# Set-up of a hybrid GLA and attention step: two weight bounds moved from VectorE to ScalarE, one row pass moved to GpSimd, set-up keys set anew

## The chip, the cores and the metric

The kernel runs on one core of one Trainium2 chip. The metric is the device time of one execution in microseconds (us). The engines are TensorE (PE, with its weight loads listed as PEld), VectorE (DVE), ScalarE (ACT), GpSimd (POOL) and SyncE (SP), which only issues transfers here.

## The reference

One inference step of two layers at model width 1024, over 256 context tokens and 1024 latent tokens. Layer 0 is a gated linear attention, layer 1 a softmax attention with grouped queries. All arithmetic is float32. Only the start of layer 0 matters here:

```python
hp = rms_norm(xp, norm_g[l]) * (1.0 + sc_p) + sh_p      # context rows
hs = rms_norm(xs, norm_g[l]) * (1.0 + sc_s) + sh_s      # latent rows

def gla_mixer(h, w_in, wa1, wa2, ba, onorm, w_out, s0):
    proj = h @ w_in
    q, k, v, gate = jnp.split(proj, [...], axis=-1)
    ...
    def decay(d):
        z = ((h @ wa1[d]) @ wa2[d] + ba[d]).astype(jnp.float32)
        return (jax.nn.log_sigmoid(z) / GLA_TAU).reshape(B, T, GLA_HEADS, GLA_DK)
```

## The kernel before

Every float32 operand of a large matmul is split into two float16 parts, hi and lo, and a product is made of three matmuls. Before a weight is split it is scaled by a power of two. That scale comes from a bound on the weight's magnitudes: the largest magnitude of each partition (`tensor_reduce` on DVE, into a small tile `wmx`), then the largest over all partitions by a small matmul on PE and a reduction of its result (`pow2`, result `p2m`, then `p2c`, `p2e`, the scale `p2s` and its inverse `p2i`).

The set-up works on three groups of row tiles of 128 tokens (`GROUPS`): four latent tiles, four more, and the two of the context. For a group, the rows' sums of squares are taken (`normalise`: a Square with an accumulator on ACT, or a product with an accumulator on DVE), POOL raises them to the power -1/2 (`rstd`, L238), the rows are scaled, PE transposes them, and ACT, DVE and POOL multiply by the conditioned gain, add the shift and split the result into `hT_hi` and `hT_lo` (`modulate`). PE then multiplies by the query and key weights of head 0 (`qk_pair`) and by the first low-rank weight (`rank`, then `rank_sum`). Names in the code: `ys` are the rows of the second group (tiles `x`), `zs` those of the context (in the buffer of `whi`, with their modulated rows in that of `wlo`), `w1` and `w2` the low-rank weights (both in one `wada` tile, split into `wa1h`, `wa1l` and `wa`), `vf` the first value weight (in `wst`), split by `fill`.

The loop over heads and row tiles (`gla`) follows, in which the value and gate products, the decays, the chunk products and the scans are interleaved, and then the attention.

A scheduler writes each engine's order. It takes the instructions by priority, and `LATER` adds a number to the priority of a named step (`later`, `placed`): negative is earlier. Names with `s.` belong to the set-up: `s.rk` splits the low-rank weights, `s.n1` normalises the second group, `s.m1` transposes and modulates it, `s.q0` and `s.q1` are the query and key products of the first and second group, `s.r0` and `s.r1` the low-rank products, `s.s0` and `s.s1` their sums, `s.v` splits the first value weight, `s.n2` normalises the context rows. All transfers into the chip that the set-up uses are issued in order on SP's queue, those of `w2` and `w1` at L585 and L587.

Of the kernel before, what the change touches and what calls it, by code (L numbers as in the profile page):

```python
# [9 lines left out]
F32 = mybir.dt.float32  # L10
I32 = mybir.dt.int32
AF = mybir.ActivationFunctionType
ALU = mybir.AluOpType
AX = mybir.AxisListType
# [3 lines left out]
P = 128  # L18
D = 1024
KT = D // P  # L20
# [6 lines left out]
GQ, GV = GH * DK, GH * DV  # L27
# [77 lines left out]
    "a0.q": 35,  # L105
    "wo3": 180,
    "x.key": -95,
    "s.v": 580,
    "s.q1": 185,
    "s.r0": -155,  # L110
    "s.n2": -490,
    "s.r1": 300,
    "gated9": 30,
    "eprep": 400,
    "x.kset": 170,
    "s.q0": -25,
    "s.s0": 45,
    "s.m1": -170,
    "s.s1": 245,
    "s.rk": -135,  # L120
    "s.n1": 0,
    "a9.val.3": -265,
    "a.s0.1": -55,
    "a9.val.1": -105,
# [36 lines left out]
class K:  # L161
# [136 lines left out]
                nc.vector.scalar_tensor_tensor(lo, par[:, q, :, b, :], so[:, b : b + 1], hi, ALU.mult, ALU.subtract)  # L298


    def fill(self, w, j, st):
        nc = self.nc
        s, w[2][j] = self.scale(st)
        h = KT // 4
        for i in range(4):
            a, n = slice(i * h, i * h + h), slice(256 * j, 256 * j + 256)
            hi, lo = w[0][:, a, n], w[1][:, a, n]
            act = nc.scalar.activation(hi, st[:, a, :], AF.Copy, scale=s)
            dve = nc.vector.scalar_tensor_tensor(lo, st[:, a, :], s, hi, ALU.mult, ALU.subtract)  # L309
        return act.ins, dve.ins  # L310
# [218 lines left out]
    def normalise(self, xs, junk, other=None):  # L529
        nc = self.nc  # L530
        n = len(xs)
        ssq = self.t(self.sm, [P, n], F32, f"nt_s{n}", bufs=2)
        for j, x in enumerate(xs):
            if other is not None and j % 2:
                nc.vector.scalar_tensor_tensor(
                    other, x, 1.0, x, ALU.mult, ALU.mult, accum_out=ssq[:, j : j + 1]
                )
            else:
                nc.scalar.activation(junk, x, AF.Square, accum_out=ssq[:, j : j + 1])
        r = self.rstd(ssq, D, f"nt_r{n}")  # L540
        for j, x in enumerate(xs):
            last = nc.vector.tensor_scalar(x, x, r[:, j : j + 1], None, ALU.mult)
        return last.ins

    def transpose(self, xs, k, tag):
# [49 lines left out]
        load(self.onorm, I["gla_onorm"].rearrange("l (j p) -> p (l j)", p=P))  # L595


    def split_rank(self, w1, w2):
        nc = self.nc
        mx = self.t(self.small, [P, 2], F32, "wmx")  # L600
        nc.vector.memset(mx, 0.0)
        nc.vector.tensor_reduce(mx[:, 0:1], w1, AX.XY, ALU.max, apply_absolute_value=True)
        nc.vector.tensor_reduce(mx[0:98, 1:2], w2, AX.XY, ALU.max, apply_absolute_value=True)
        s, inv = self.pow2(mx, 2)
        hi = self.t(self.gcp, [P, KT, 32], F16, "wa1h")
        lo = self.t(self.gcp, [P, KT, 32], F16, "wa1l")
        nc.scalar.activation(hi, w1, AF.Copy, scale=s[:, 0:1])
        nc.vector.scalar_tensor_tensor(lo, w1, s[:, 0:1], hi, ALU.mult, ALU.subtract)
        self.wa1 = hi, lo

        nc.scalar.activation(self.wa2, w2, AF.Copy, scale=s[0:98, 1:2])
        low = self.wa2[64:98]
        nc.vector.scalar_tensor_tensor(low, w2[64:98], s[64:98, 1:2], low, ALU.mult, ALU.subtract)
        nc.scalar.activation(self.wa2[96:97], w2[96:97], AF.Copy, scale=s[96:97, 1:2])
        self.inv_rank = self.t(self.gcp, [P, 2], F32, "inv_rk")
        nc.vector.tensor_copy(self.inv_rank, inv)

# [971 lines left out]
def run(job):  # L1589
    return job[0](*job[1:])  # L1590
# [3 lines left out]
def emit(ctx, tc, I, O, dbg=None, stop=None):  # L1594
    k = K(ctx, tc, I, O, dbg)
    nc = tc.nc
# [27 lines left out]
    with ExitStack() as c:  # L1624
# [9 lines left out]
        with ExitStack() as c1:  # L1634
            k.p1 = k.pool("p1", ctx=c1)
            k.hw = k.p1
            small = nc.scalar.dma_start
            rows = k.t(k.p1, [40, P], F32, "rows")
            small(rows[0:8, :], I["c_ctx"].rearrange("(k p) -> k p", p=P))
            small(rows[8:16, :], I["c"].rearrange("b (k p) -> (b k) p", p=P))  # L1640
            small(k.ident, I["k_ident"])
            small(rows[16:24, :], I["norm_g"][0].rearrange("(k p) -> k p", p=P))
            small(rows[24:40, :], I["b_ada"][0, 0 : 2 * D].rearrange("(k p) -> k p", p=P))

            def group(gi):
                xs = []
                for j in range(GROUPS[gi][1]):
                    x = k.t(k.p1, [P, D], F32, "x", bufs=4)
                    load(x, xrow(I, GROUPS[gi][0] + j))
                    xs.append(x)  # L1650
                return xs

            xs = group(0)
            wq = k.wtile(0)
            qk = k.load_qk(wq, 0)
            to = []
            for t in (*k.wtile(1)[0:2], *k.wtile(2)[0:2], k.hT_hi, k.hT_hi, k.hT_lo, k.hT_lo):
                a = 4096 * (len(to) % 2) if len(to) > 3 else 0
                t = t.rearrange("p k n -> p (k n)")[:, a : a + 4096].bitcast(F32)
                n = len(to)  # L1660
                for b in ((0, 2 * D),) if n < KT - 1 else ((0, D), (D, 2 * D)):
                    load(t[:, slice(*b)], I["w_ada0"][n, :, slice(*b)])
                to.append(t)
            w = k.gla_consts()
            k.cond_vectors(rows)
            junk = k.t(k.p1, [P, D], F16, "junk")
            last = k.normalise(xs, junk)
            xT = k.t(k.p1, [P, KT, 512], F32, "xT")
            for kk in range(KT):
                nc.vector.tensor_copy(xT[:, kk, :], k.transpose(xs, kk, ("z", "mm")[kk % 2]))  # L1670
            k.mod_rows(to[0:NEAR], 0)
            with tc.issue_after(last):
                run(qk)
                cross = k.cross
            k.gla_tables()
            ys = group(1)
            wv = k.wtile(1)
            vf = k.load_v(wv, 0)
            k.spare = k.bank("U")
            step = cross  # L1680
            for n in range(NEAR, KT):
                with tc.issue_after(step):
                    k.mod_rows(to[n : n + 1], n)
                if n < KT - 1:
                    step = k.idle_steps(6, k.mod_mm)
            k.mod_cols()
            step = k.idle_steps(6, k.mod_mm)
            late = [t.rearrange("p k n -> p (k n)").bitcast(F32) for t in k.wtile(2)[0:2]]
            zs = [late[0][:, D * j : D * j + D] for j in range(2)]
            for j, x in enumerate(zs):  # L1690
                load(x, xrow(I, GROUPS[2][0] + j))
            with tc.issue_after(step):
                k.gs, k.sh, k.inv_h = k.affine()
            step = k.idle_steps(16, k.cross)
            for kk in range(KT):
                act, dve = k.modulate(xT[:, kk, :], kk, GROUPS[0][0], kk % 2 == 0)
            k.fold_qk(0, wq)
            with tc.issue_after(act.ins), tc.issue_after(dve.ins):
                with k.later("s.rk"):
                    k.split_rank(*w)  # L1700
                    k.rank_scales()
                k.placed("s.n1", k.normalise, ys, junk, k.t(k.p1, [P, D], F16, "junk2"))
            with tc.issue_after(step):
                k.placed("s.q0", k.qk_pair, 0, 0, wq)
            nxt = k.placed("s.r0", k.rank, 0)
            with k.later("s.m1"):
                for kk in range(KT):
                    act, dve = k.modulate(
                        k.transpose(ys, kk, banks[kk % 6]), kk, GROUPS[1][0], kk % 2 == SECOND
                    )  # L1710
            first = dve.ins
            with tc.issue_after(act.ins), tc.issue_after(first):
                k.placed("s.v", run, vf)
                k.placed("s.n2", k.normalise, zs, junk)
            k.placed("s.q1", k.qk_pair, 0, 1, wq)
            k.placed("s.s0", k.rank_sum, *nxt)
            k.placed("s.s1", k.rank_sum, *k.placed("s.r1", k.rank, 1))
            late_qk = k.load_qk(wq, 1)
# [135 lines left out]
def xrow(I, i):  # L1854
    if i < NTP:
        return I["x_prompt"][0, i * P : i * P + P, :]
    return I["x_sample"][0, (i - NTP) * P : (i - NTP) * P + P, :]
# [97 lines left out]
```

## Time and profile before

| | us |
|---|---|
| median of 3 runs | 1243.88 (1243.77 to 1244.47) |
| the profiled execution | 1240.44 |
| its span, first to last instruction | 1238.7 |
| PE busy | 1190.6 (96%) |
| DVE busy | 941.7 (76%) |
| ACT busy | 684.6 (55%) |
| POOL busy | 323.7 (26%) |
| mean granted TensorE clock | 0.997 of full speed |

Times in the profile are counted from the span's start. A line such as L602 is one of the kernel before; in the new kernel the same statements stand 4 to 25 lines further down. A name on the left of an arrow is the tile written, those on the right are read. A PE row's end is modelled, so rows of PE that follow each other can overlap by a little.

### The profile page before, as it was taken

To read this page: it belongs to the slowest core of one execution; us is meant where nothing else is said; L and a number is where in the kernel's file an instruction comes from. 1 tells how busy PE (TensorE), PEld (TensorE's weight loads), DVE (VectorE), ACT (ScalarE), POOL (GpSimd) and SP (SyncE) were. 2 spreads that over 40 slices of the span, in tenths; PEclk is the share of its full clock that TensorE was granted. 3 is DMA by queue.
4 is the path that set the end of the run, shared out by engine and by line. 5 is a ranking of instruction groups with operands and counts; after the bars stand their busy time and mean duration, and the time that the engine had idled before them with its cause. 6 is when DMAs were issued, how large, how long until landed. Compare 5 with 4: busy or idle time off the path is not lost. (4 is left out here: it accounts for less than half of the span.)

```text
span 1238.7 us, 22382 instructions
## 1 busy us (share of the span) xinstructions
PE 1190.6 (96%) x7990; PEld 779.1 (63%) x7990; DVE 941.7 (76%) x2177; ACT 684.6 (55%) x1694; POOL 323.7 (26%) x566
## 2 busy tenths in 40 slices
PE   5899999999999999799999999999999999989998
PEld 3467765655556566567776666766766667766444
DVE  4787778888788789986876877877767687796653
ACT  3574565666666657742333576666677676663100
POOL 0132122333221243310223444331332342310000
PEclk9999999999999999999999999999999999999999
DMA  9511567366555544479987896667957666889442
GB/s 381 215 48 74 196 195 237 113 198 203 175 186 171 184 136 144 124 189 308 205 192 187 186 174 137 134 132 145 191 126 156 128 118 137 193 152 240 153 136 85
DMA packets 318496, 210.14 MB, mean 170 GB/s; under 512 B 257158, under 2 KB 294702, under 8 KB 310064
## 3 DMA queue, kind: packets, MB, share of 16 engines
q1 hardware_dynamic: 311232, 191.18, 60.2%
q10 hardware_dynamic: 4688, 10.57, 2.3%
q0 software_dynamic: 2464, 6.95, 2.0%
q8 instruction: 63, 1.03, 0.4%
q14 instruction: 49, 0.40, 0.1%
HBM read 108.35 MB, written 38.96 MB: 119 GB/s over the span
## 5 line engine op out<-in xcount | busy, mean ns | idle before, releaser
L247 PEld LDWEIGHTS <-hT_hi 128*128 128x128 f16 x1920 | 187.6, 98 | 119.9 <-issue 3.8
L247 PE MATMUL mm<-whi,hT_hi 128*128 128x512 f16 (+1 forms) x576 | 200.1, 348 | 3.1 <-ACT gx L718 2.7
L247 PE MATMUL mm<-whi,hT_lo 128*128 128x512 f16 (+1 forms) x576 | 200.2, 347 | 0.0
L247 PE MATMUL mm<-wlo,hT_hi 128*128 128x512 f16 (+1 forms) x560 | 194.2, 347 | 0.7 <-DVE wlo L309 0.7
L247 PEld LDWEIGHTS <-whi 128*128 128x128 f16 x1232 | 120.2, 98 | 60.3 <-issue 0.9
L1344 PE MATMUL S<-kT,wst 128*128 128x512 f16 (+1 forms) x624 | 142.1, 338 | 6.5 <-ACT p L1352 6.5
L247 PE MATMUL mm<-hT_hi,whi 128*128 128x256 f16 (+1 forms) x480 | 141.0, 294 | 0.6 <-DVE og L1407 0.6
L247 PE MATMUL mm<-hT_lo,whi 128*128 128x256 f16 (+1 forms) x480 | 141.0, 294 | 0.0
L247 PE MATMUL mm<-hT_hi,wlo 128*128 128x256 f16 (+1 forms) x480 | 141.0, 294 | 0.0
L1382 DVE SCALAR_TENSOR_TENSOR phl<-p,srec,phl 128x1280 f16<-128x1280 f32 (+1 forms) x79 | 105.5, 1335 | 45.7 <-ACT phl L1381 28.4
L247 PEld LDWEIGHTS <-hT_lo 128*128 128x128 f16 x960 | 94.2, 98 | 61.3 <-issue 0.9
L1347 DVE TENSOR_REDUCE smx<-S 128x1 f32<-128x1280 f32 (+1 forms) x80 | 101.5, 1272 | 27.3 <-PE S L1344 27.1
L247 PE MATMUL mm<-PT,vh 128*128 128x256 f16 x672 | 114.8, 273 | 5.8 <-DMA PT<-phl 5.6
L1352 ACT ACTIVATE p<-S,snb,acol 128x1280 f32<-128x1280 f32 (+1 forms) x80 | 99.0, 1238 | 8.9 <-DVE phl L1382 3.8
L1344 PEld LDWEIGHTS <-wst 128*128 128x128 f16 x624 | 61.0, 98 | 57.0 <-issue 7.7
L247 PE MATMUL mm<-PT,vl 128*128 128x256 f16 x336 | 91.6, 273 | 0.0
L1379 POOL TENSOR_SCALAR phl<-p,srec 128x1280 f16<-128x1280 f32 (+1 forms) x40 | 53.7, 1342 | 104.6 <-DVE srec L1370 57.8
L247 PEld LDWEIGHTS <-wlo 128*128 128x128 f16 x616 | 60.2, 98 | 29.4
L247 PEld LDWEIGHTS <-vh 128*128 128x128 f16 x672 | 65.2, 98 | 16.0 <-DMA PT<-phl 4.4
L1172 POOL TENSOR_TENSOR rope<-hx,ropet 128x64 f32<-128x64 f32 x160 | 53.9, 367 | 76.2 <-ACT hx L1308 61.9
L270 DVE TENSOR_REDUCE wmx<-wst 128x1 f32<-128x512 f32 x104 | 65.2, 677 | 7.4 <-DMA wst<-in_att_w 5.2
L238 POOL TENSOR_TENSOR hrs<-hrsa,mhalf 128x2 f32<-128x2 f32 x50 | 40.1, 803 | 102.8 <-DVE hrsa L236 84.9
(383 smaller groups left out, 2681.0 us busy)
## 6 DMA issues: line engine op xcount, KB each, us to landing
wada<-in_w_ada SPq DMA_DIRECT2D x16, 1024.0 KB, 5.4
wst<-in_att_w SPq DMA_DIRECT2D x14, 1024.0 KB, 5.5
wst<-in_gla_w_in SPq DMA_DIRECT2D x12, 1024.0 KB, 5.5
og_d<-og POOLq DMA_DIRECT2D x40, 128.0 KB, 2.8
wst<-og_d SPq DMA_DIRECT2D x5, 1024.0 KB, 6.5
og_d<-gx SPq DMA_DIRECT2D x37, 128.0 KB, 2.1
xr<-x_d SPq DMA_DIRECT2D x9, 512.0 KB, 3.4
out<-xr ACTq DMA_DIRECT2D x17, 256.0 KB, 2.0
```

What stands on the lines that cost most here:

```text
L238: nc.gpsimd.tensor_tensor(r, a, self.mhalf[:, 0:w], ALU.pow)
L247: self.pe = self.nc.tensor.matmul(out, a, b, start=k == 0 and j == 0, stop=k == n - 1 and j == 2).ins
L270: nc.vector.tensor_reduce(mx[:, j : j + 1], st[:, 2 * j : 2 * j + 2, :], AX.XY, ALU.max, apply_absolute_value=True)
L1172: nc.gpsimd.tensor_tensor(tv[:, h, :, w, :], xv[:, h, :, 1 - w, :], sn[:, :, w, :], ALU.mult)
L1344: nc.tensor.matmul(S[:, a : a + n], x, y, start=m == 0, stop=m == 2)
L1347: last = nc.vector.tensor_reduce(mx, S, AX.X, ALU.max).ins
L1352: nc.scalar.activation(p, S, AF.Exp, scale=self.sexp, bias=nb, accum_out=den)
L1379: nc.gpsimd.tensor_scalar(hi, p, r, 2.0 ** 14, ALU.mult, ALU.mult)
L1382: nc.vector.scalar_tensor_tensor(lo, p, r2, hi, ALU.mult, ALU.subtract)
```

## The change

The low-rank weights and the first value weight get their bound from ACT: it takes the absolute value with an accumulator, which gives each partition's sum of magnitudes instead of its largest. A sum is never smaller than the largest term, so it is a bound too. The low-rank bounds stand as a step of their own (`s.rb`), emitted ahead of the modulation of the first group; those of the value weight (`row_sums`, `s.vb`) are two sums that one DVE addition joins. In the second group POOL scales the third of four row tiles. The split of the second low-rank weight (`s.w2`) and the scales (`s.rs`) have keys of their own, and the keys of the set-up steps are set anew.

```diff
@@ LATER
-    "s.v": 580,
+    "s.v": 530,
...
+    "s.vb": 115,
+    "s.rb": 395,
...
+    def row_sums(self, st, junk):
+        mx = self.t(self.small, [P, 4], F32, "wmx")
+        h = KT // 2
+        for j in range(2):
+            f = st[:, h * j : h * j + h, :].rearrange("p k n -> p (k n)")
+            self.nc.scalar.activation(junk, f, AF.Abs, accum_out=mx[:, j : j + 1])
+        m = self.t(self.small, [P, 1], F32, "wm1")
+        self.nc.vector.tensor_tensor(m, mx[:, 0:1], mx[:, 1:2], ALU.add)
+        return m
+
-    def fill(self, w, j, st):
+    def fill(self, w, j, st, m=None):
         nc = self.nc
-        s, w[2][j] = self.scale(st)
+        s, w[2][j] = self.scale(st) if m is None else self.pow2(m)
...
         for j, x in enumerate(xs):
-            last = nc.vector.tensor_scalar(x, x, r[:, j : j + 1], None, ALU.mult)
+            if other is not None and j == 2:
+                nc.gpsimd.tensor_scalar(x, x, r[:, j : j + 1], 1.0, ALU.mult, ALU.mult)
+            else:
+                last = nc.vector.tensor_scalar(x, x, r[:, j : j + 1], None, ALU.mult)
...
+    def rank_bounds(self, w1, w2, junk):
+        nc = self.nc
+        mx = self.t(self.p1, [P, 2], F32, "rmx", bufs=1)
+        nc.gpsimd.memset(mx, 0.0)
+        for j, (t, n, w) in enumerate(((w1, P, 32 * KT), (w2, 98, 2 * GQ))):
+            f = t.rearrange("p a b -> p (a b)")
+            nc.scalar.activation(junk[0:n, 0:w], f, AF.Abs, accum_out=mx[0:n, j : j + 1])
+        self.rmx = mx
+
     def split_rank(self, w1, w2):
         nc = self.nc
-        mx = self.t(self.small, [P, 2], F32, "wmx")
-        nc.vector.memset(mx, 0.0)
-        nc.vector.tensor_reduce(mx[:, 0:1], w1, AX.XY, ALU.max, apply_absolute_value=True)
-        nc.vector.tensor_reduce(mx[0:98, 1:2], w2, AX.XY, ALU.max, apply_absolute_value=True)
-        s, inv = self.pow2(mx, 2)
+        s, inv = self.pow2(self.rmx, 2)
...
-        nc.scalar.activation(self.wa2, w2, AF.Copy, scale=s[0:98, 1:2])
-        low = self.wa2[64:98]
-        nc.vector.scalar_tensor_tensor(low, w2[64:98], s[64:98, 1:2], low, ALU.mult, ALU.subtract)
-        nc.scalar.activation(self.wa2[96:97], w2[96:97], AF.Copy, scale=s[96:97, 1:2])
+        with self.later("s.w2"):
+            ...
...
+            k.placed("s.rb", k.rank_bounds, *w, junk)
...
                 with k.later("s.rk"):
                     k.split_rank(*w)
+                with k.later("s.rs"):
                     k.rank_scales()
...
-                k.placed("s.v", run, vf)
+                m = k.placed("s.vb", k.row_sums, vf[3], junk)
+                k.placed("s.v", run, (*vf, m))
```

What the new keys do to the order, at three places. DVE between the bounds of the low-rank weights (`wmx`) and the scaling of the second group's rows (`x_300` is the first, `junk` with `nt_s` the statistics of a row tile). Before:

```order
L602 TENSOR_REDUCE wmx_455<-wada_154 128x1
L603 TENSOR_REDUCE wmx_455<-wada_154 98x1
L535 SCALAR_TENSOR_TENSOR junk_113_497,nt_s_114_498<-x_306 128x1024
L210 TENSOR_REDUCE p2m_462<-o_459 128x2
L236 TENSOR_SCALAR nt_r4a_503<-nt_s_114_498 128x4
L214 TENSOR_SCALAR p2c_464<-p2m_462 128x2
L216 TENSOR_SCALAR p2e_466<-p2c_464 128x2
L218 TENSOR_SCALAR p2s_468<-p2e_466 128x2
L220 TENSOR_SCALAR p2i_470<-p2e_466 128x2
L616 COPY inv_rk_479<-p2i_470 128x2
L226 TENSOR_TENSOR inv_r_481<-invh_85_401,inv_rk_479 128x1
L542 TENSOR_SCALAR x_300<-x_300,nt_r_116_505 128x1024
```

And now, on the same engine at the same place:

```order
L549 SCALAR_TENSOR_TENSOR junk_113_497,nt_s_114_498<-x_306 128x1024
L218 TENSOR_SCALAR p2c_464<-p2m_462 128x2
L240 TENSOR_SCALAR nt_r4a_503<-nt_s_114_498 128x4
L220 TENSOR_SCALAR p2e_466<-p2c_464 128x2
L222 TENSOR_SCALAR p2s_468<-p2e_466 128x2
L224 TENSOR_SCALAR p2i_470<-p2e_466 128x2
L639 COPY inv_rk_479<-p2i_470 128x2
L230 TENSOR_TENSOR inv_r_481<-invh_86_405,inv_rk_479 128x1
L646 TENSOR_SCALAR sr_483<-inv_r_481 128x1
L630 SCALAR_TENSOR_TENSOR wa1l_473<-wada_154,p2s_468,wa1h_472 128x256
L650 TENSOR_SCALAR one_485<-inv_r_481 128x1
L559 TENSOR_SCALAR x_300<-x_300,nt_r_116_505 128x1024
```

The two reductions are gone, the reduction into `p2m` has moved ahead of the last statistics pass, and the split into `wa1l` has moved ahead of the rows' scaling.

PE behind the products of the first group. Before, the cross-partition matmuls of the low-rank bound and the first low-rank matmul stand ahead of the second group's transposes:

```order
L686 MATMUL mm_512<-hT_lo_74,whi_23_126 128x512
L205 LDWEIGHTS wmx_455
L205 MATMUL o_459<-ident_81,wmx_455 128x128
L205 LDWEIGHTS wmx_455
L205 MATMUL o_459<-ident_81,wmx_455 128x128
L647 LDWEIGHTS wa1h_472
L647 MATMUL mm_565<-hT_hi_73,wa1h_472 32x512
L548 MATMUL z_592<-ident_81,x_300 128x128
L548 MATMUL cs_601<-ident_81,x_300 128x128
```

And now:

```order
L709 MATMUL mm_512<-hT_lo_74,whi_23_126 128x512
L565 MATMUL z_592<-ident_81,x_300 128x128
L565 MATMUL cs_601<-ident_81,x_300 128x128
L565 MATMUL A_610<-ident_81,x_300 128x128
L565 MATMUL kt_619<-ident_81,x_300 128x128
L565 MATMUL U_628<-ident_81,x_300 128x128
L565 MATMUL o_637<-ident_81,x_300 128x128
```

The cross-partition matmuls stand ahead of the first group's products now. The transposes of the first row tile come next, then all low-rank matmuls, and the transposes of the three other tiles behind those; before, those of two tiles came ahead of the low-rank matmuls.

ACT from the second group's queries on (`q`, `k` are the products' copies, `r` a scaled low-rank sum, `h` the copy of a low-rank product, `wlo` a modulated piece of the context rows, `ls` a step of the decay, `whi` the value weight's hi part). Before:

```order
L673 ACTIVATE q_152_750<-mm_700,iqk_94_451 128x512
L673 ACTIVATE k_153_752<-mm_701,iqk_95_453 128x512
L660 ACTIVATE r_143<-mm_754,sr_483 96x512
L564 ACTIVATE wlo_75_377<-U_950,gb_76_380 128x256
L652 COPY h_156_783<-mm_758 96x512
L738 ACTIVATE ls_800<-z_798,inv_z_493 128x256
L564 ACTIVATE wlo_75_377<-U_962,gb_76_380 128x256
L564 ACTIVATE wlo_75_377<-o_944,gb_76_380 128x256
L739 ACTIVATE ls_800<-ls_800 128x256
L308 ACTIVATE whi_70_308<-wst_310,p2s_679 128x2x256 x4
```

And now:

```order
L696 ACTIVATE q_152_748<-mm_698,iqk_95_455 128x512
L696 ACTIVATE k_153_750<-mm_699,iqk_96_457 128x512
L581 ACTIVATE wlo_76_381<-U_948,gb_77_384 128x256
L581 ACTIVATE wlo_76_381<-o_942,gb_77_384 128x256
L322 ACTIVATE whi_70_308<-wst_310,p2s_677 128x2x256 x4
L683 ACTIVATE r_143<-mm_752,sr_483 96x512
L581 ACTIVATE wlo_76_381<-U_960,gb_77_384 128x256
L581 ACTIVATE wlo_76_381<-o_954,gb_77_384 128x256
L675 COPY h_156_781<-mm_756 96x512
L581 ACTIVATE wlo_76_381<-U_972,gb_77_384 128x256
L581 ACTIVATE wlo_76_381<-o_966,gb_77_384 128x256
L761 ACTIVATE ls_798<-z_796,inv_z_493 128x256
```

The value weight's split has moved ahead of the first low-rank sum's scaling and of the copy of the second low-rank product.

More of the change, by code (lines that the diff above doesn't have):

```diff
@@ L107 @@
     "x.key": -95,
-    "s.v": 580,
[L109 to L112, printed above, removed]
+    "s.v": 530,
+    "s.q1": 240,
+    "s.r0": -220,
+    "s.n2": -645,
+    "s.r1": 240,
     "gated9": 30,
@@ L115 @@
     "x.kset": 170,
[L116 to L121, printed above, removed]
+    "s.q0": -20,
+    "s.s0": -45,
+    "s.m1": 120,
+    "s.s1": 150,
+    "s.rk": -325,
+    "s.vb": 115,
+    "s.rb": 395,
+    "s.rs": -115,
+    "s.w2": 0,
+    "s.n1": -360,
     "a9.val.3": -265,
@@ L609, in split_rank @@
         self.wa1 = hi, lo
-        nc.scalar.activation(self.wa2, w2, AF.Copy, scale=s[0:98, 1:2])
-        low = self.wa2[64:98]
-        nc.vector.scalar_tensor_tensor(low, w2[64:98], s[64:98, 1:2], low, ALU.mult, ALU.subtract)
-        nc.scalar.activation(self.wa2[96:97], w2[96:97], AF.Copy, scale=s[96:97, 1:2])
+        with self.later("s.w2"):
+            nc.scalar.activation(self.wa2, w2, AF.Copy, scale=s[0:98, 1:2])
+            low = self.wa2[64:98]
+            nc.vector.scalar_tensor_tensor(low, w2[64:98], s[64:98, 1:2], low, ALU.mult, ALU.subtract)
+            nc.scalar.activation(self.wa2[96:97], w2[96:97], AF.Copy, scale=s[96:97, 1:2])
         self.inv_rank = self.t(self.gcp, [P, 2], F32, "inv_rk")
```

## The prediction

> **What bounds the kernel now.** I read the busy time by stage first. Its columns are the stretch, its length, then busy time and instruction count of PE, PEld, DVE, ACT and POOL, the granted TensorE clock, the DMA share and GB/s.
>
> ```profile
> 49.30:60.30 11.00, 7.60 (x55) 5.12 (x54) 7.54 (x25) 6.00 (x9) 1.63 (x2) 0.84 0.04 6
> 71.70:79.20 7.50, 6.33 (x42) 2.74 (x43) 5.10 (x16) 5.63 (x12) 1.48 (x3) 1.00 0.00 0
> 79.20:140.00 60.80, 60.72 (x481) 46.35 (x481) 45.87 (x116) 35.98 (x89) 15.59 (x34) 1.00 0.29 103
> 500.00:1239.00 739.00, 716.58 (x4970) 486.83 (x4968) 541.21 (x1094) 389.82 (x956) 192.25 (x326) 1.00 0.73 164
> ```
>
> From 79.2 to 140 PE is busy without a gap (60.72 of 60.80 us), and the change adds and removes no PE work. PE idles later (22.4 us after 500), but there in an unchanged order behind work that moves along with it. So a set-up that ends earlier ends the kernel earlier by the same amount, and the change is worth what it takes out of PE's idle time before 79.2: of the 3.40 us in the first of these stretches and the 1.17 us in the second. Next I read the timeline of those two (start, duration, engine, line, operation; in brackets the idle time before and what ended it).
>
> ```profile
> 47.09 0.41 DVE L602 TENSOR_REDUCE wmx<-wada 128x1 f32<-128x256 f32 x1
> 47.42 1.21 DVE L603 TENSOR_REDUCE wmx<-wada 98x1 f32<-98x1024 f32 x1
> 48.55 1.21 DVE L535 SCALAR_TENSOR_TENSOR junk<-x 128x1024 f16<-128x1024 f32 x1
> 49.69 0.42 DVE L210 TENSOR_REDUCE p2m<-o 128x2 f32<-128x256 f32 x1
> 50.27 1.01 POOL L238 TENSOR_TENSOR nt_r<-nt_r4a,mhalf 128x4 f32<-128x4 f32 x1 [4.97 <-DVE nt_r4a L236]
> 50.76 0.51 ACT L607 ACTIVATE wa1h<-wada,p2s 128x256 f16<-128x256 f32 x1 [0.23 <-DVE p2s L218]
> 51.32 0.39 PE L647 MATMUL mm<-hT_hi,wa1h 128*32 128x512 f16 x1 [1.76 <-ACT wa1h L607]
> 51.32 1.42 DVE L542 TENSOR_SCALAR x<-x,nt_r 128x1024 f32<-128x1024 f32 x2
> 52.13 0.47 PE L548 MATMUL z<-ident,x 128*128 128x128 f32 x1 [0.42 <-DVE x L542]
> 52.71 0.47 DVE L608 SCALAR_TENSOR_TENSOR wa1l<-wada,p2s,wa1h 128x256 f16<-128x256 f32 x1
> 53.17 1.41 DVE L542 TENSOR_SCALAR x<-x,nt_r 128x1024 f32<-128x1024 f32 x2
> 54.61 1.29 DVE L613 SCALAR_TENSOR_TENSOR wa<-wada,p2s,wa 34x1024 f16<-34x1024 f32 x1
> 57.02 0.58 ACT L652 COPY h<-mm 96x512 f32<-96x512 f32 x1 [4.71 <-PE mm L647]
> 57.62 1.14 ACT L614 ACTIVATE wa<-wada,p2s 1x1024 f16<-1x1024 f32 x1
> 58.79 0.78 ACT L564 ACTIVATE h<-z,gb 128x512 f32<-128x512 f32 x1
> 59.62 0.55 PE L548 MATMUL z<-ident,x 128*128 128x128 f32 x3 [1.19 <-ACT h L564]
> ```
>
> Here is a DVE chain: bounds of the low-rank weights, statistics of the second group's rows, the power on POOL, the rows scaled, and only then PE's transposes. ACT closes it: its modulation of the second group starts at 58.79, and PE waits 1.19 us for its first output. I call 58.79 point A. The stretch also runs at half clock for a while:
>
> ```profile
> 51.80:55.40 3.60, 3.27 (x18) 2.67 (x21) 3.57 (x8) 0.50 (x1) 0.00 (x0) 0.53 0.00 0
> ```
>
> **The low-rank bounds (L602, L603 gone from DVE).** ACT now sums magnitudes ahead of its first modulation. The bound is a larger number than the maximum, which alters a scale and no instruction's size. The nearest price is that of a Square with an accumulator over 1024 elements, and this is where the sums would go:
>
> ```profile
> 63.06 1.05 ACT L539 ACTIVATE junk<-whi 128x1024 f16<-128x1024 f32 x1
> 64.01 0.20 ACT L539 ACTIVATION_READ_ACCUMULATOR junk<-whi 128x1 f32 x1
> 36.96 0.81 ACT L561 ACTIVATE hT_hi<-xT,gb 128x512 f16<-128x512 f32 x1 [4.52 <-DVE invh L493]
> 19.37 0.36 SPq L587 DMA_DIRECT2D wada<-in_gla_wa  x1
> wada<-in_gla_wa SPq DMA_DIRECT2D x1, 128.0 KB, 15.0
> ```
>
> One such pass takes 1.05 us, and 0.20 more for reading the accumulator; two of them, one only 256 wide and so nearer the 0.51 of L607, make 1.9 us. ACT idles 4.52 us ahead of its first modulation. The second weight tile was issued at 19.37 and landed 15.0 us later, at 34.4. So the sums would run from 34.4 to 36.3, 0.65 us before the modulation at 36.96 that is queued behind them on ACT. I cost them at nothing; without that cover they delay ACT, and PE with it, one for one. The maximum's cross-partition matmuls go ahead of PE's first long run and cost it under 0.1 us.
>
> DVE gains 0.41 + 1.21 less overlap: its second statistics pass started 1.46 us after the first reduction did (48.55 against 47.09). In the new order only the 0.42 us reduction of the PSUM result stands there, so the pass starts about 1.05 us earlier, at 47.5. That reduction no longer stands behind the pass, so the power on POOL starts 1.25 us earlier, at 49.0, and ends at 50.0.
>
> **The row scaling, and one row tile on POOL.** Two things eat into this gain. First, DVE now splits the low-rank weight (0.47 us) ahead of the rows, so the first row tile would be scaled from 50.6 to 51.3; it ended at 52.05 before. Second, POOL scales the third tile at the same time. Price of that pass, from both sides:
>
> ```profile
> L565 POOL TENSOR_SCALAR hT_hi<-h 128x512 f16<-128x512 f32 x8 | 5.6, 709 | 44.1 <-ACT h L564 44.1
> L1379 POOL TENSOR_SCALAR phl<-p,srec 128x1280 f16<-128x1280 f32 x32 | 48.9, 1528 | 82.7 <-DVE srec L1370 52.1 <-DMA PT<-phl 29.1 <-ACT ls L352 1.4
> 87.09 0.52 POOL L747 TENSOR_SCALAR ghi<-g 128x256 f16<-128x256 f32 x1 [0.36 <-DVE g L743]
> 87.26 0.62 DVE L764 TENSOR_TENSOR en<-en,k 128x256 f32<-128x256 f32 x1
> 93.34 0.42 DVE L764 TENSOR_TENSOR en<-en,k 128x256 f32<-128x256 f32 x1
> ```
>
> Between 0.71 us for 512 columns and 1.53 for 1280, 1024 columns take about 1.25 us. POOL's pass itself is hidden, since PE now transposes that tile only after the low-rank matmuls. But DVE's product took 0.62 us beside a POOL pass and 0.42 without: POOL's remaining 0.35 us cost DVE 0.20. So beside 1.25 us DVE loses between nothing and 1.25; I take 0.8, near the rows' proportion. Then the first tile is ready at 52.1 (no earlier than before) and the last of DVE's three at 53.5 instead of 54.58, one pass of 0.7 having left DVE. The Trainium skill, SBUF — State Buffer, section "Who interferes with whom", says that DVE with two SBUF inputs, or in a two-port mode, and a reading GpSimd instruction exclude each other for a whole instruction; by that DVE would lose the whole 1.25 and the sum below would be 0.85 us. The rows agree in kind.
>
> From there to A: PE transposes the first tile only, six at the half-clock step of 0.215 (52.1 to 53.4), then runs the low-rank matmuls, partly still at half clock, until about 56.1; before, the copy of their result began at 57.02. On DVE the split of the second weight (1.29 us) ends at 55.1; ACT's one-row pass (1.14) ends at 56.3, now ahead of the copy (0.58), which runs 56.4 to 57.0. A moves from 58.79 to 57.0: a gain of 1.8 us. Its bounds are 1.35 with DVE held for the whole pass, 2.35 with DVE not held, and 2.8 if the clock does not halve either.
>
> **The first value weight.** The rows of this step:
>
> ```profile
> 66.27 0.78 ACT L564 ACTIVATE h<-z,gb 128x512 f32<-128x512 f32 x1 [0.36 <-DVE hT_lo L566]
> 68.59 1.07 POOL L238 TENSOR_TENSOR nt_r<-nt_r2a,mhalf 128x2 f32<-128x2 f32 x1 [0.83 <-DVE nt_r2a L236]
> 69.01 2.46 DVE L270 TENSOR_REDUCE wmx<-wst 128x1 f32<-128x512 f32 x4
> 71.39 1.40 DVE L542 TENSOR_SCALAR whi<-whi,nt_r 128x1024 f32<-128x1024 f32 x2
> 71.78 1.10 PE L658 MATMUL mm<-h,sum 96*96 96x512 f32 x2
> 72.92 0.68 ACT L660 ACTIVATE r<-mm,sr 96x512 f16<-96x512 f32 x1 [0.54 <-PE mm L658]
> 76.79 0.56 ACT L564 ACTIVATE wlo<-o,gb 128x256 f32<-128x256 f32 x1
> 77.55 2.56 ACT L308 ACTIVATE whi<-wst,p2s 128x512 f16<-128x512 f32 x4
> 79.28 0.27 PE L247 MATMUL mm<-wlo,hT_hi 128*128 128x256 f16 x1 [0.69 <-DVE wlo L309]
> ```
>
> DVE loses four reductions (2.46 us); they lay beside PE's matmuls. ACT gains two sums of 1.05 and 0.2 each in the middle of the modulation, with the Square of the prompt rows, the last modulation and the second Square queued behind them. The last modulation moves from A + 7.5 to A + 8.3; PE's matmuls want its output at about A + 10, so I cost that at nothing. Then, counted from A: second Square to 10.25, POOL's power (1.07) to 11.8, prompt rows scaled (1.40) to 13.25, where before it was 14.0; PE's transposes wait for them some 0.5 us; ACT's two passes of 0.56 to 15.2; the weight's split (2.56) to 17.6. But in the new order this split stands ahead of the scaling of the first low-rank sum (0.68), two modulation passes and the copy of the second low-rank product (0.58). Those now end at 19.7, and PE's second sum (1.10) waits for that copy and ends at 20.85. The first value matmuls follow. Before, the run of value matmuls starts at 79.28 less one matmul of 0.11, or A + 20.4. So the v step loses 0.45 us against A, by a chain of a dozen rows; I keep 0 and 1.0 as its ends. Behind it the decays' first cumulative sums come after some 3 us of value matmuls instead of 6, and ACT and DVE reach them about 0.5 us ahead.
>
> **Sum.** 1.8 less 0.45 is about 1.3 us. The profiled execution took 1240.44 us (span 1238.7 and 1.7 around it) and would take 1239.1; it lies 3.4 us below the median of the runs, 1243.88, to which I apply the same difference: 1242.6 us.
>
> **Rivals.**
>
> The clock falls again in the v step. PE ends its transposes at A + 13.6, its first sum (1.10) at 14.7 and, by an estimate, the low-rank matmuls with transposes between them at 17.0; then it idles about 1.8 us for the passes behind the split. In the second stretch the clock fell after 1.76 us of idle time and one matmul, to 0.53 over 3.6 us. The same here costs about half of 3 us, 1.5 us: 1244.1. Against it: whether a stall is seen depends on where it falls. The Trainium skill, TensorE: Matmul & The Clock Gate, Part 1, has the clock fall after an idle window of about 3.4 us, free-running; by that alone it would stay up here, and the sum stays 1.3. The trace shows a fall after a shorter stall, so I give this rival a chance all the same.
>
> DVE is not held by POOL's pass: A gains 2.35, time 1242.0. For it: nothing in the trace overlaps just these forms.
>
> More idle time goes: no holding, the first stall at full clock (A gains 2.8) and the v step at its end of 0: 2.8 us, 1241.1. For it: half a dozen instructions fewer before the first transposes. Against it: PE still stands 2 us before them.
>
> The sums are late (the other side). If the low-rank weights land after 35.05, ACT's first modulation waits behind the sums, and everything after it. Past 36.4 the kernel is slower than before, past 38.8 by over 2.5 us: 1246.4 and more. For it: the larger tile's landing is not in the trace. Against it: it was issued ahead of the other on the same queue.
>
> An ACT pass in front of a bank's release: in the first slots the next head's weight split (2.56 us) now stands ahead of the copy that frees a PSUM bank, with some 0.2 us to spare; 1.5 us lost gives 1244.1.
>
> **How the numbers follow.** As summed 0.36 (1242.6); clock falls 0.16 (1244.1); DVE not held 0.14 (1242.0); more idle time goes 0.22 (1241.1); sums late 0.08 (over 1246.4); bank 0.04 (1244.1). I forecast 1242.6. The range 1240.6 to 1245.0 leaves out the late sums, the lowest part of the case at 1241.1 and the worst of the two at 1244.1. Two runs of this kernel can be told apart at 0.2%, 2.5 us, so faster means below 1241.4: most of that case and a tail of the unheld one, 0.25. Slower, over 1246.4: the late sums and a tail of the bank, 0.10. Within: 0.65.
>
> **What would show it.** Right: A near 57.0, value matmuls from 77.9, DVE's scaling rows over 0.75 us beside POOL's pass, the first modulation still at 37.0. Wrong: A below 56.4 or not earlier at all, a clock of 0.5 after 75, PE gaps past 80, or a modulation after 37.5.

## The result, and the profile after

| | median (us) | runs | ratio to before, 95% interval |
|---|---|---|---|
| before, beside it | 1244.52 | 22 | |
| changed kernel | 1241.53 | 22 | 0.9973 (0.9963 to 0.9984) |
| changed kernel, timed a second time | 1242.16 (before 1243.02) | 12 (17) | 1.0001 (0.9983 to 1.002) |

Faster by 3.4 us on the first occasion and by nothing on the second; the two intervals weighted together give about 2.5 us, 1.4 to 3.6 (worked out from the two). The ratios are those on record; the plain quotient of the second pair of medians is 0.9993, or 0.9 us. 1241.53 lies in the predicted range, 1.1 us under the predicted time, but that range (1240.6 to 1245.0) held the time of the kernel before as well, so lying in it says little.

The profiled execution of the changed kernel took 1243.01 us (span 1241.2), longer than the one of before (1240.44), which lay 3.4 us under its own median. So the two spans tell nothing, and positions are compared instead. The first modulation is the best zero: it waits for the last conditioning weight and came at 36.96 us before and at 36.8 to 39.1 in the runs below, with every kernel. In none of them did it wait for the new sums on ScalarE.

The busy time by stage of the changed kernel, in the columns of the prediction's first fence:

```profile
49.30:60.30 11.00, 8.57 (x63) 5.15 (x62) 8.06 (x23) 7.21 (x10) 2.78 (x3) 0.84 0.25 89
71.70:79.20 7.50, 6.99 (x51) 3.33 (x50) 6.66 (x13) 7.25 (x15) 2.95 (x6) 1.00 0.28 93
79.20:140.00 60.80, 60.80 (x498) 46.22 (x496) 44.39 (x113) 34.88 (x87) 14.63 (x33) 1.00 0.28 98
500.00:1241.00 741.00, 719.37 (x4960) 487.79 (x4958) 540.22 (x1094) 388.95 (x955) 192.81 (x326) 0.99 0.72 163
```

PE idles 2.43 us in the first stretch (3.40 before) and 0.51 in the second (1.17). The third is as full as before, but 498 matmuls pass in it instead of 481: a first hint, no more, of something that the prediction had not counted. The timeline of the changed kernel, with the rows that answer to those of before:

```profile
34.75 0.42 ACT L621 ACTIVATE junk<-wada 128x256 f16<-128x256 f32 x1 [1.74 <-DMA wada<-in_gla_wa]
35.30 1.06 ACT L621 ACTIVATE junk<-wada 98x1024 f16<-98x1024 f32 x1
37.54 0.81 ACT L578 ACTIVATE hT_hi<-xT,gb 128x512 f16<-128x512 f32 x1 [1.10 <-DVE invh L507]
48.00 1.22 DVE L549 SCALAR_TENSOR_TENSOR junk<-x 128x1024 f16<-128x1024 f32 x1
49.59 1.02 POOL L242 TENSOR_TENSOR nt_r<-nt_r4a,mhalf 128x4 f32<-128x4 f32 x1 [3.71 <-DVE p2e L220]
50.71 1.14 POOL L557 TENSOR_SCALAR x<-x,nt_r 128x1024 f32<-128x1024 f32 x1
50.84 2.87 DVE L559 TENSOR_SCALAR x<-x,nt_r 128x1024 f32<-128x1024 f32 x3
52.45 0.33 PE L565 MATMUL z<-ident,x 128*128 128x128 f32 x1 [2.43 <-DVE x L559]
55.20 1.14 ACT L637 ACTIVATE wa<-wada,p2s 1x1024 f16<-1x1024 f32 x1 [2.66 <-DVE wa L636]
56.84 0.58 ACT L675 COPY h<-mm 96x512 f32<-96x512 f32 x1 [0.50 <-PE mm L670]
57.45 0.78 ACT L581 ACTIVATE h<-z,gb 128x512 f32<-128x512 f32 x1
71.94 2.56 ACT L322 ACTIVATE whi<-wst,p2s 128x512 f16<-128x512 f32 x4
76.87 1.02 PE L681 MATMUL mm<-h,sum 96*96 96x512 f32 x2
77.73 0.27 PE L251 MATMUL mm<-whi,hT_hi 128*128 128x256 f16 x1
```

Counted from the first modulation, point A comes at 19.91 instead of 21.83 (1.92 us earlier) and the run of value matmuls at 40.19 instead of 42.21 (2.02 earlier). The three rows on DVE take 2.87 us; the first ends at 52.39, so it took 1.55.

Behind the set-up, PE's rows of the third low-rank product (24 matmuls, each with 32 columns of weights) look different. First the kernel before:

```profile
108.20 0.28 PE L647 MATMUL mm<-hT_lo,wa1h 128*32 128x256 f16 x1
108.41 0.28 PE L247 MATMUL mm<-whi,hT_hi 128*128 128x256 f16 x1
108.63 0.28 PE L647 MATMUL mm<-hT_hi,wa1h 128*32 128x256 f16 x1
108.84 0.28 PE L247 MATMUL mm<-wlo,hT_hi 128*128 128x256 f16 x1
```

And the changed kernel:

```profile
107.39 0.27 PE L251 MATMUL mm<-whi,hT_hi 128*128 128x256 f16 x1
107.50 0.27 PE L251 MATMUL mm<-wlo,hT_hi 128*128 128x256 f16 x1
107.71 0.28 PE L670 MATMUL mm<-hT_hi,wa1h 128*32 128x256 f16 x1
107.71 0.28 PE L670 MATMUL mm<-hT_hi,wa1l 128*32 128x256 f16 x1
107.71 0.28 PE L670 MATMUL mm<-hT_lo,wa1h 128*32 128x256 f16 x1
107.83 0.27 PE L670 MATMUL mm<-hT_hi,wa1h 128*32 128x256 f16 x1
```

Left together, three narrow matmuls start at once and the next three 0.11 us later (107.71, 107.83). Interleaved with full-width ones each change of width takes a step of 0.215 instead of 0.108, so a change costs 0.107 us. PE's order has 18 such changes in this product before and 4 in the changed kernel. A narrow matmul between full-width ones also has a step to itself that three could share. From the first of the 24 to the next work behind them PE took 4.09 us before, with 8 other matmuls in between, and 1.52 us in the changed kernel, with 2; at 0.108 us for each of the others, the product itself took 3.2 and 1.3 us. The Trainium skill, TensorEngine Tiling (Array Packing), section "Key Properties", says that a change of the tiling mode drains TensorE while a change of tile does not; the rows agree that a change costs, 0.107 us here, and show neither a drain nor its absence.

### The profile page after: what moved, and what is told of

Its sections match the earlier page's. It is cut to its first block, busy times and chain, and to the rows that moved or that the text cites. A ratio compares the mean times of both kernels' runs of the same rounds, so it can differ in the third digit from the quotient of the medians.

```text
span 1241.2 us, 22376 instructions
## 1 busy us (share of the span) xinstructions
PE 1194.1 (96%) x7990; PEld 780.3 (63%) x7990; DVE 937.9 (76%) x2169; ACT 688.3 (55%) x1702; POOL 324.6 (26%) x568
## 3 DMA queue, kind: packets, MB, share of 16 engines
HBM read 108.35 MB, written 38.96 MB: 119 GB/s over the span
## 5 line engine op out<-in xcount | busy, mean ns | idle before, releaser
L274 DVE TENSOR_REDUCE wmx<-wst 128x1 f32<-128x512 f32 x100 | 62.7, 678 | 6.1 <-DMA wst<-in_att_w 3.4
```

The lines of the kernel that those rows point to most:

```text
L274: nc.vector.tensor_reduce(mx[:, j : j + 1], st[:, 2 * j : 2 * j + 2, :], AX.XY, ALU.max, apply_absolute_value=True)
```

## The experiments

Transposes, point A and value matmuls are in us after the first modulation. A lead "at 130", "at 190" or "at 440" is how much earlier PE's matmuls around that time of the profile of before came, each kernel counted from its own first modulation. "Changes" are those of width in the third low-rank product, counted in PE's order; "half" says whether the clock halved in or right behind PE's stall. About 1.0 us of each lead at 440 is the loss of the kernel before itself: in its profiled execution PE waited 0.83 us at 221 us, which most of the others did not.

| kernel | transposes | point A | value matmuls | half | changes | at 440 | median (us) | ratio to before, 95% |
|---|---|---|---|---|---|---|---|---|
| before | 15.17 | 21.83 | 42.21 | yes | 18 | 0 | 1244.5, 1243.0 to 1243.5 | |
| changed | 14.91 | 19.91 | 40.19 | yes | 4 | 3.2 | 1241.53 | 0.9973 (0.9963 to 0.9984) |
| after_again | 14.91 | 19.70 | 39.99 | yes, later | 4 | 4.2 | 1242.16 | 1.0001 (0.9983 to 1.002) |
| before_grouped | 15.17 | 22.00 | 42.37 | yes | 2 | 1.6 | 1241.08 | 0.9979 (0.9961 to 0.9997) |
| before_grouped2 | 15.17 | 21.98 | 42.36 | yes | 2 | 2.7 | 1241.40 | 0.9978 (0.996 to 0.9996) |
| after_grouped | 14.90 | 19.90 | 40.18 | yes | 2 | 4.4 | 1243.37 | 0.999 (0.9974 to 1.0006) |
| after_split | 14.92 | 19.43 | 39.72 | no | 12 | 1.8 | 1244.54 | 1.001 (0.9993 to 1.0026) |
| g_dverow | 14.10 | 18.68 | 38.96 | no | 2 | 4.4 | 1241.52 | 0.9978 (0.9958 to 0.9999) |
| a_actrow3 | 14.11 | 18.64 | 38.92 | no | 4 | 5.1 | 1240.68 | 0.9967 (0.9953 to 0.9981) |
| g_idle | 14.93 | 19.45 | 39.73 | no | 2 | 3.7 | 1240.81 | 0.9981 (0.9965 to 0.9998) |
| g_idle_actrow3 | 14.10 | 18.63 | 38.90 | no | 2 | 4.1 | 1238.98 | 0.9967 (0.9948 to 0.9986) |
| a_dverank | 14.98 | 22.58 | 43.84 | past A | 20 | -1.9 | 1259.94, one run | |
| a_dveval | 14.91 | 19.43 | 39.81 | no | 18 | 3.4 | 1256.66, one run | |
| b_newkeys | 14.98 | 20.93 | 41.39 | no | 18 | 1.1 | 1247.23, one run | |

**The order of the third low-rank product.** On the kernel before:

```diff
-                k.rank_sum(*k.rank(2, h[0]))
+                k.rank_sum(*k.placed("s.r2", k.rank, 2, h[0]))      # "s.r2": -60
```

> The kernel before, with one key more: the third low-rank product is placed 60 ahead, so its 24 matmuls (32 weight columns each) stand together on PE instead of one by one between full-width matmuls. Set-up as before. Order theory: each change between a narrow and a full-width matmul costs PE 0.107 us (step 0.215 against 0.108); 18 changes become 2, so the first head's later matmuls (after 130 us, counted from the first modulation) come 1.7 us earlier than before and the median is 1.7 us lower (1.2 to 2.2). Idle theory (only PE's idle time ahead of the value matmuls counts): within 0.3 us of before, in the trace and in the median.

The set-up is untouched (point A 22.00), PE is 2.1 us ahead at 130 us, and the median 2.5 us lower, a little beyond the expected 1.2 to 2.2. SP's order is the one of before, and no row differs behind 166 us, so nothing else moved later. The 24 narrow matmuls take 0.99 us together instead of 3.2: the saving is 2.2 us, of which the expectation had priced the changes (1.7) and not the shared steps (some 0.5). The same kernel again:

> The kernel before with its third low-rank product kept together, timed again beside the next one, which has the same product kept together and the changed set-up. Both theories: 1.7 us below before at the first head, ratio near 0.998; low-rank product and point A as in before (point A 21.4 to 22.0 us after the first modulation).

Ratio 0.9978, after 0.9979. So this order alone is worth about what the whole change is, and none of it lies in the set-up. The idle theory falls. The opposite, the changed kernel with the key at +60:

> The changed kernel with the third low-rank product placed 60 later: 12 changes between narrow and full-width matmuls instead of 4; the set-up up to the value matmuls as in the changed kernel. Order theory: 8 times 0.107 us, PE 0.9 us later than the changed kernel after 130 us, so about 2.0 us faster than before instead of 2.9. Idle theory: as the changed kernel, 2.9 us faster than before.

With 12 changes PE is 2.1 us ahead of before at 130 us where the changed kernel is 3.1 ahead: 1.0 us, as the order theory has it. But the median is as before's, where both theories had it lower. This kernel is no clean test: the key moved rows up to 569 us too, SP's queue among them, and PE has 2.6 us of waits at 537 to 553 us (0.50, 0.64, and 1.45 for `gx`) where the changed kernel has none.

**POOL's row pass.** The third tile back on DVE, then on ScalarE (behind the first keys; the order behind the set-up stays the changed kernel's):

```diff
-            if other is not None and j == 2:
-                nc.gpsimd.tensor_scalar(x, x, r[:, j : j + 1], 1.0, ALU.mult, ALU.mult)
-            else:
+            # g_dverow: all four on DVE ("s.r2": -60 as well)
+            # a_actrow3: for j == 2  nc.scalar.activation(x, x, AF.Copy, scale=r[:, j : j + 1])
```

> The changed kernel with the third row tile of the second group scaled on DVE again instead of POOL, and the third low-rank product kept together (2 changes). Holding theory (POOL's pass holds DVE about as long as it relieves it): DVE's rows take 0.745 us each; the first transposes come 14.1 us after the first modulation (14.9 in the changed kernel), the last of the four rows is ready at 16.3 (16.2), and point A is within 0.5 us of the changed kernel's 19.9, rather earlier than later: 19.5. Relief theory: POOL takes 0.75 us off DVE, so without it point A is at 20.6.

> The changed kernel with the third row tile scaled on ScalarE (after the first keys, where it waits anyway) instead of POOL; the order behind the set-up is the changed kernel's. Holding theory: DVE's rows go back to 0.745 us, the first transposes come 14.1 us after the first modulation (14.9), point A at 18.7 (at half clock 19.0) instead of 19.4 (at half clock 19.9). Relief theory (what matters is that DVE has three rows and not four): 14.9, and point A unchanged.

The timeline of a_actrow3, whose first modulation is at 37.30:

```profile
50.61 2.07 DVE L559 TENSOR_SCALAR x<-x,nt_r 128x1024 f32<-128x1024 f32 x3
51.41 0.33 PE L565 MATMUL z<-ident,x 128*128 128x128 f32 x1 [1.62 <-DVE x L559]
52.20 1.14 ACT L557 ACTIVATE x<-x,nt_r 128x1024 f32<-128x1024 f32 x1
55.94 0.78 ACT L581 ACTIVATE h<-z,gb 128x512 f32<-128x512 f32 x1
```

Three rows take 2.07 us without POOL beside them and 2.87 with it: POOL's 1.14 us hold DVE for 0.80. In g_dverow all four take 2.73, less than three beside POOL. The holding theory is right on the rows and the first transposes (14.1 in both) and, in a_actrow3, to 0.06 us on point A. In g_dverow it was too kind to the pass: point A at 18.68 where 19.5 was expected, about 0.5 of it because the clock stayed up. At full clock point A is at 18.65 without the pass and at 19.43 with it (after_split, a_dveval). POOL's pass makes the set-up 0.8 us longer. The time of g_dverow is no clean test of this, since its keys moved rows up to 323 us and SP's queue as well; in a_actrow3 nothing differs behind 59 us, but its ratio, 0.9967, lies within the interval of the changed kernel.

**The half clock.** Dummy matmuls in PE's stall (they write a spare bank that nothing reads):

```diff
+ k.placed("s.q0", k.idle_steps, 18, k.qk_last)      # behind k.qk_pair(0, 0, wq); "s.r2": -60 as well
```

> The changed kernel with 18 dummy matmuls of 256 columns (1.9 us, no input or output of the kernel) in PE's idle time ahead of the second group's transposes, and the third low-rank product kept together. Clock theory: PE's clock halves because of that idle time; with the dummies it stays at 1.0, the six transposes step by 0.108 instead of 0.215 and the low-rank product ends some 1.6 us earlier. Point A then moves by only 0.5 us, to 19.4 after the first modulation, since ScalarE's one-row pass (ending 18.8) stands ahead of the copy (0.58). If the half clock itself set point A: 18.3. If the halving has another cause than idle time: clock 0.5 again, point A at 19.9.

Of g_idle, the dummies and the first transpose, then the stretch behind them:

```profile
50.28 2.13 PE L400 MATMUL U<-ident 128*128 128x256 f16 x18
52.89 0.33 PE L565 MATMUL z<-ident,x 128*128 128x128 f32 x1 [0.48 <-DVE x L559]
```

```profile
52.90:57.00 4.10, 4.10 (x43) 2.83 (x44) 3.69 (x9) 1.40 (x3) 0.00 (x0) 1.00 0.00 0
```

Clock 1.00 and point A at 19.45, as expected. But the dummies are not needed for that: the same set-up with the same stall of 2.43 us halved the clock in the changed kernel (first row) and not in after_split (second):

```profile
53.50:55.50 2.00, 2.00 (x17) 0.75 (x18) 1.90 (x6) 0.30 (x1) 0.00 (x0) 0.50 0.00 0
```

```profile
53.50:55.50 2.00, 1.49 (x18) 0.98 (x21) 1.97 (x6) 0.60 (x2) 0.00 (x0) 1.00 0.00 0
```

Point A: 19.91 and 19.43. So the clock is worth 0.48 us here. After_grouped and after_again, with this stall too, fell; a_dveval didn't.

What decides can be read from the traces. In each of them the stretches at half clock begin on one grid of 3.413 us (in the kernel before at 51.89 and 499.04, 131 steps apart) and last whole steps, but for one that the profile's end cuts. The clock fell when one step of the grid held much of the stall: PE idled 2.43 us in the step ahead of the fall in the changed kernel, 2.42 in after_grouped, 2.00 in after_again and 1.95 in the kernel before. In after_split and a_dveval the grid cuts the same stall in two, 1.07 and 1.36 us, 1.41 and 1.02 us, and the clock stayed; so it did in a_actrow3 and g_dverow, whose stall is 1.62 us. Over all fourteen traces, from 25 us on, every step with 2.0 us or more of idle time was followed by half clock, and no fall from full clock followed less than 1.5 us; in between both happened. What is left to chance is where the grid lies against the stall. This is read from the runs as they fell; no edit here moved a stall against the grid.

**The set-up alone, and everything together.** after_grouped is the changed kernel with "s.r2": -60; g_idle_actrow3 has that key, the third row on ScalarE and 14 dummies:

> The changed kernel with its third low-rank product kept together (2 changes between narrow and full-width matmuls instead of 4). Against the kernel before with the same product kept together only the set-up differs. Theory that the set-up's gain reaches the end: point A 2.0 to 2.5 us earlier, the matmuls up to 440 us 2.0 to 2.5 us earlier, and the median 2.0 us lower. Rival, that it is waited away later (a weight's landing at about 460 us): the same lead at 440 us, but medians within 0.7 us of each other.

> All that helped so far in one kernel: the changed kernel, third row tile on ScalarE, 14 dummy matmuls of 256 columns (1.5 us) ahead of the second group's transposes, third low-rank product kept together. Expected: clock 1.0 throughout, first transposes at 14.1, point A at 18.7, 3.2 us ahead of before at point A and 4.9 at 200 us, counted from the first modulation; median 0.7 us below the changed kernel if the gain reaches the end, equal to it if it is waited away.

after_grouped leads before_grouped2 by 2.1 us at point A and by 1.7 us at 440 us, and yet its median is 2.0 us higher, with intervals that overlap. Neither theory had named that: here the set-up's lead did not show at the end. g_idle_actrow3 came out as expected at point A (18.63), but PE then waits 1.48 us for POOL's `ghi` at 144 us, and it leads by 3.0 at 190 us and by 4.1 at 200 us after the first modulation, where 4.9 was expected; its median is the lowest of all, 2.6 us under the changed kernel's first. It beats the kernel before (0.9967, 9 runs); that it beats the changed kernel lies within the two intervals.

**The parts.** The low-rank bound on DVE again; the value bound on DVE again; the kernel before with the eleven changed keys alone:

```diff
# a_dverank
-            k.placed("s.rb", k.rank_bounds, *w, junk)
...  in split_rank, with a new tile mx:
+        nc.vector.tensor_reduce(mx[:, 0:1], w1, AX.XY, ALU.max, apply_absolute_value=True)
+        nc.vector.tensor_reduce(mx[0:98, 1:2], w2, AX.XY, ALU.max, apply_absolute_value=True)
# a_dveval
-                m = k.placed("s.vb", k.row_sums, vf[3], junk)
-                k.placed("s.v", run, (*vf, m))
+                k.placed("s.v", run, vf)
```

> The changed kernel with the low-rank weights bounded by DVE's reductions again (0.41 and 1.21 us, now behind both statistics passes and ahead of the power). One look: positions counted from the first modulation. If the bound's move carries the set-up's gain: first transposes at 16.0 (14.9 in the changed kernel, 15.2 before), point A at 21.4 (at half clock 21.9), so no gain left there. Rival, that the keys carry it: point A under 20.

> The changed kernel with the first value weight bounded by DVE's four reductions (2.46 us) again. One look. Point A as in the changed kernel (19.4, at half clock 19.9). If the sums on ScalarE carry the value step: value matmuls 0.5 to 1.0 us later against point A (A + 20.8 to 21.3 instead of A + 20.3). If they only take work off an engine that waits: A + 20.3.

> The kernel before with the eleven changed keys alone (no sums on ScalarE, no pass on POOL). One look. If the keys need the freed DVE: value matmuls at 42.2 or later after the first modulation (42.2 before, 40.2 in the changed kernel). If the keys carry the gain: 40.2 to 41.

With the new keys and POOL's pass in place, the low-rank sums carry the set-up: without them point A is at 22.58, 0.7 us beyond the expected 21.9 and 3.15 behind the 19.43 that the changed set-up has at full clock (the clock of a_dverank fell only behind point A). The kernel before with the keys alone, so without the sums and without POOL's pass, has point A at 20.93 and its value matmuls at 41.39, 0.8 us earlier than before and between both expectations. But its clock stayed up and before's fell, which was worth 0.48 us in the changed kernel, so how much of the 0.8 is the keys' is not shown. The value sums bring 0.1 us at most: without them the value matmuls come at A + 20.38, as before, with them at A + 20.28.

The times of the first two were not expected at all: one execution each, 17 and 14 us slower than the median of before. Up to 500 us nothing points to it. Then, in a_dveval, PE and SP:

```profile
579.55 0.59 PE L251 MATMUL kv<-whi,hT_hi 128*128 128x256 f16 x2 [10.95 <-DMA whi<-w_kv]
573.75 0.73 SPq L1145 DMA_DIRECT2D whi<-w_kv  x1
```

And SP in the changed kernel:

```profile
560.38 0.53 SPq L1145 DMA_DIRECT2D whi<-w_kv  x1
```

The next layer's K/V weight is issued 13 us later, behind transposes and transfers that stood behind it, and PE waits 10.95 us for it. In a_dverank it is issued at 571.05. An edit at 62 us had moved a row of SP's queue at 560, since the order is set for the whole program at once.

**The changed kernel again.**

> The changed kernel once more, timed beside before, since the same kernel with its third low-rank product kept together came out 1.7 us slower than its first median though it leads at 440 us. Theory that these medians scatter by 1 to 1.5 us from later stalls: 1240.5 to 1242.5, ratio 0.9970 to 0.9985. If the 1241.2 of its first runs was low by chance: 1242.5 to 1243.

1242.16 us lies in the first theory's range, but the ratio, 1.0001, does not lie in its 0.9970 to 0.9985, so the two theories are not told apart. Its profile leads by 4.2 us at 440.

Where do such leads go? The clearest place is at 460 us. Here is DVE in the kernel before (first fence) and in the changed kernel (second), waiting for the same weight:

```profile
461.61 1.87 DVE L270 TENSOR_REDUCE wmx<-wst 128x1 f32<-128x512 f32 x3 [0.23 <-DMA wst<-in_gla_w_in]
455.89 0.49 SPq L262 DMA_DIRECT2D wst<-in_gla_w_in  x1
```

```profile
460.45 1.87 DVE L274 TENSOR_REDUCE wmx<-wst 128x1 f32<-128x512 f32 x3 [1.70 <-DMA wst<-in_gla_w_in]
453.27 0.49 SPq L266 DMA_DIRECT2D wst<-in_gla_w_in  x1
```

The issue kept the lead (2.62 us of profile time, 3.2 counted from the first modulation), but the transfer took 7.2 us instead of 5.7, and 1.35 us of PE's lead were gone. DVE waited as long there in g_dverow (2.21 us) and g_idle (1.94); a_actrow3 lost nothing there. Over the nine kernels with the changed kernel's or before's later order, the profiled executions lost 1.6 to 7.2 us between 440 and 1225 us against before's one, 4.3 in the mean (the 7.2 is b_newkeys). Before's execution lay 3.4 us under its first median and 2.6 to 4.1 under the four in the table, which is most of that. The medians say the same: the eight of these kernels that have a ratio gained 2.5 us in the mean by it, against a mean lead of 3.6 at 440, of which 1.0 is before's own loss. So in the mean the leads seem to be kept, with single executions some 2 us around them; for no single kernel is it shown, and after_grouped speaks against it. In after_again, the very same kernel, the load took 5.5 us, so the change is not what lengthened it; why a transfer takes longer in one execution stays open.

## Why the prediction was right, and where it was not

- **Low-rank sums hidden: right.** They end at 36.45; the modulation at 37.54 waits for DVE, as it did, and is late by 0.58 for a conditioning weight that landed late. "A modulation after 37.5" was a sign of being wrong; at 37.54 it appeared, but not from the sums: ScalarE stood idle for the 1.10 us before it.
- **DVE's second pass and POOL's power earlier: right.** The power starts 12.05 us after the first modulation instead of 13.31: 1.26 earlier, 1.25 predicted.
- **DVE held for 0.8 us: right, 0.80**, beside a pass of 1.14 us instead of 1.25. The Trainium skill, SBUF — State Buffer, section "Who interferes with whom", has it held for a whole instruction. The rows fit that better than I read it: POOL's pass ran from 50.71 to 51.85, DVE's first row began 0.13 behind it and ended 0.54 after it, so the row took as long as if it had done next to nothing while the pass ran; the price is less than the pass's 1.14 by the head start and by what of the row's own 0.745 (some 0.2, an estimate from these two rows) passes before its data. What I didn't do is price the set-up without the pass: "the last of DVE's three at 53.5 instead of 54.58, one pass of 0.7 having left DVE" books the pass as relief, and it costs 0.8.
- **Point A: right in its size, with another last wait.** 1.92 us earlier, 1.8 predicted with the half clock that the run had. The prediction has ScalarE's one-row pass end last, at 56.3, just behind PE's low-rank matmuls at 56.1. That pass ended at 56.34 with everything 0.58 later, so 0.5 us sooner than predicted, and the copy then waited 0.50 us for PE, whose low-rank matmuls ran at half clock. That two estimates so close gave the right sum is partly luck; at full clock the pass does come last (after_split), and point A is at 19.43.
- **The v step: mis-sized.** I had it lose 0.45; it lost nothing (A + 20.28 after, 20.38 before). The weight's split started at A + 14.5 where I had 15.2, since PE's two transposes and ScalarE's passes follow the scaled rows without the waits that I had added link by link. The end of its range, 0, was the value.
- **What failed: "a set-up that ends earlier ends the kernel earlier by the same amount", with work behind it "in an unchanged order".** PE's order differs up to matmul 1062 of 7990, at 162 us. The third low-rank product has 14 changes of width fewer, 1.5 us by their price, and took 1.9 us less by its rows; PE's lead grows from 2.0 us at the value matmuls to 2.9 at 190 us, so about 1.0 of the 1.9 was lost again elsewhere in the new order, and where is not shown. before_grouped shows that such an order alone, with no gain in the set-up, is worth 0.9979 and 0.9978. I had the changed order at hand and read it only up to the value matmuls.
- **Clock falling in the v step** (a rival at 0.16): in no run. **ScalarE's pass ahead of a bank's release, sums late**: in no run.

In sum: 2.0 us of set-up where 1.3 were forecast (mostly the v step), 0.9 more from the order behind it, less what later waits take at random. That the time came out 1.1 us from the forecast is the balance of these, and not a confirmation of 1.3.

## What to carry to other kernels

Where a scheduler orders the whole program, an edit in one place is an edit everywhere: compare the order on PE and on the transfer queue to the end, count changes between narrow and full-width matmuls, and look for loads that moved behind other work; an edit in the set-up cost some 15 us here that way, twice. Before a pass is given to POOL to relieve DVE, set its length times the share that it holds (0.80 of 1.14 us here) against the row that DVE saves (0.66): ScalarE took the same pass without holding DVE's rows (2.07 us for three), though point A was no earlier than with all four on DVE (18.64 and 18.68). And a gain of 2 us in a program whose executions scatter by 2 is shown by positions in the trace, counted from an event that both kernels share, not by one pair of times.

## What the runs showed of the hardware that was not expected

- Three matmuls with 32 columns of weights run in the time of one (0.108 us for 256 elements) if they are neighbours; each change to or from full width costs 0.107 us. 24 of them took 0.99 us together and 3.2 among full-width ones.
- After the same stall of 2.43 us the clock halved in three executions and not in two. Where it fell, here and in four others, it stayed down for 3.41 to 3.42 us (summed over windows of 0.5 us). The falls lie on a grid of 3.413 us, and every step of it with 2.0 us or more of PE's idle time was followed by one. The Trainium skill, TensorE: Matmul & The Clock Gate, Part 1, describes a window of 3.413 us that runs freely; the grid and the length agree with that. That the clock falls only after a whole idle window doesn't: no stall of the set-up was as long, and before it fell after 1.76 us and one matmul.
- The same 1 MB load took 5.7 us from issue to landing in the kernel before and 7.2 in the changed kernel, and 5.5 in after_again, the same kernel; over the fourteen traces it took 5.4 to 7.7.
